# First products of a hybrid encoder layer: low parts on VectorE in order of need, K halves of both units in turn, the queries' low part in both partition halves

## The chip, the cores and the metric

The kernel runs on one core of a Trainium2 chip. The metric is the time of one execution on the device in microseconds; three executions of the kernel before took 883.92, 884.14 and 884.91 us (median 884.14). The core has TensorE (PE, matrix products; its weight loads are a row of their own, PEld), VectorE (DVE), ScalarE (ACT), GpSimd (POOL) and SyncE (SP), which here only issues DMAs. Each engine works through its own instructions in order, and semaphores order them against each other.

## The reference

One encoder layer over 512 positions of width 1024. The normalised input h is multiplied once by a wide matrix `w_in` whose columns feed four token mixers (a short convolution, a stick-breaking attention, an RWKV-7 recurrence, a gMLP gate) and four gates; the sum of the gated mixers goes through `w_o`, and a gated feed-forward part with a short convolution follows. Cut to what matters here:

```python
def stick_breaking_attention(q, k, v):
    ...
        z = jnp.einsum('bhqd,bhkd->bhqk', qi, kh).astype(jnp.float32) * scale
    ...

def hybrid_mixer(h, w_in, ...):
    proj = h @ w_in
    y_a = short_conv_mixer(proj[..., SC_OFF:SB_OFF], sc_conv_w)
    q, k, v = jnp.split(proj[..., SB_OFF:RW_OFF], 3, axis=-1)
    y_b = stick_breaking_attention(q.reshape(hs), k.reshape(hs), v.reshape(hs))
    y_c = rwkv7_mixer(proj[..., RW_OFF:SG_OFF], ...)
    y_d = spatial_gating(proj[..., SG_OFF:GATE_OFF], sg_ln_g, sg_ln_b, sg_w, sg_b)
    ...

def reference(x, mix_norm_g, w_in, ...):
        h = rms_norm(x, mix_norm_g[l])
        x = x + hybrid_mixer(h, w_in[l], ...)
        h = rms_norm(x, ffn_norm_g[l])
        x = x + conv_glu_ffn(h, w_up[l], ffn_conv_w[l], w_down[l])
    return rms_norm(x, final_norm_g)
```

Everything is float32.

## The kernel before

**Products in three parts.** Each operand is split into a high part (`whi`, `hH`: the value cast to a shorter form) and a low part (`wlo`, `hL`: the value less its high part). `mm3` (lines 168 to 172) makes a product of three matmuls: high x high (L169), high x low (L170), low x high (L171), and then calls `tick()`. The cast of `split` (L100) stands on ACT, the difference (L101) on DVE unless another engine is named.

**Weights.** A unit is 256 columns of a weight matrix with all 1024 rows (K). It comes in four pieces of 128 partitions x 512 numbers; piece n holds the rows of K tiles 2n and 2n + 1. SP issues the DMAs in program order (`raw`), ACT and DVE make `whi` and `wlo`.

**First products.** x is 4 tiles of 128 positions (tile 0 to 3). `mix_stats` makes the row sums of squares on ACT in two halves (L181), their sum (L185), root (L187) and inverse (L189). For tiles 0 and 1, PE transposes x against a diagonal of the inverses (L287); `mix_gain` multiplies the result by the norm's weights (`hf`, L238, DVE), and `split` makes hH and hL from it, K half by K half (half 0 is K tiles 0 to 3). For tiles 2 and 3, ACT scales x first (`xn`, L305), and the thread `mix_rest` transposes it later (L314) between the products: `WN` = 19 ticks after the start for tile 2, `WN2` = 5 more for tile 3. `gemm2_halves` multiplies two units, `first` (columns RW0 + 768) and `second` (RW0 + 256 and RW0), first with tiles 0 and 1 (t2_ = 0), then with tiles 2 and 3; in each token half all of the first unit's K comes ahead of the second unit's. The low parts of the first unit's four pieces are made on POOL (`split(*first[0][0], pool)` and so on), all others on DVE.

The order on PE is the program's; in the block around these lines (`manual_schedule` with three engines) so it is on ACT and DVE, except that instructions from outside the block may be put between. Everything else on ACT, DVE and POOL is ordered by the scheduler of the language.

**Queries, keys and scores.** For a pair j of heads, `qS[j]` holds the scaled high part of the queries of head hp in both partition halves, `kS[j]` the high part of the keys in the head's own half and their low part in the other one, so that one matmul of 128 rows gives high x high and low x high (L931). `qL[j]` holds the queries' low part in the own half alone, and a matmul of 64 rows adds high x low (L932); a third one of 128 columns adds the mask (L933). These twelve matmuls of a head, over 512, 384, 256 and 128 columns, are its score block; there are four.

## Time and profile before

| | |
|---|---|
| median of three executions | 884.14 us |
| the profiled execution | 885.09 us |
| its span, first to last instruction | 883.4 us |
| PE busy | 865.9 us (98%) |
| DVE / ACT / POOL busy | 506.0 / 413.2 / 18.9 us |
| mean granted clock of TensorE | 0.992 |

The span is what the trace shows; the execution has 1.7 us around it. Matmuls overlap, so a row's duration is longer than the distance to the next row's start, and distances of starts are what counts on PE. The granted clock is 1.00 at the higher of TensorE's two levels (2.4 GHz) and 0.50 at the lower (1.2 GHz).

### The profile page before, as it was taken

What the parts mean: (1) busy time and instruction counts of PE and PEld (TensorE: products, weight loads), DVE (VectorE), ACT (ScalarE), POOL (GpSimd) and SP (SyncE); (2) the same over time, 40 slices, a digit from 0 to 9 for tenths busy, and PEclk for the clock granted to TensorE, in tenths of its full rate; (3) what the DMA queues carried; (4) which work ended last, traced back from release to release, by engine and by line L of the source; (5) the groups of instructions that cost most, each with busy time, mean ns of one, the idle gap of its engine ahead of it and who ended that gap; (6) DMA issues with size and microseconds to landing.
All of it is one profiled execution on the core that took longest, in us unless ns stands there. A gap on an engine that the chain in (4) does not pass through costs nothing.

```text
span 883.4 us, 12631 instructions
## 1 busy us (share of the span) xinstructions
PE 865.9 (98%) x4767; PEld 709.8 (80%) x4767; DVE 506.0 (57%) x868; ACT 413.2 (47%) x676; POOL 18.9 (2%) x61
## 2 busy tenths in 40 slices
PE   6999999999999999999999999999999999999997
PEld 6978877788778788888888898888888888888876
DVE  5577747875364555544554676634665366634645
ACT  7473345643344587765344554413443144413425
POOL 6000000000000000000000000000000000000000
PEclk9999999999999999999999999999999999999999
DMA  7223331233133322226336252314432063314102
GB/s 242 63 83 99 86 97 49 63 87 97 52 86 93 99 62 65 73 62 200 96 96 182 69 167 96 96 37 117 134 96 84 8 183 107 96 37 131 36 1 95
DMA packets 102773, 82.20 MB, mean 93 GB/s; under 512 B 12716, under 2 KB 92152, under 8 KB 102712
## 3 DMA queue, kind: packets, MB, share of 16 engines
q1 hardware_dynamic: 102040, 79.82, 30.4%
q10 hardware_dynamic: 592, 1.31, 0.5%
q8 instruction: 37, 0.61, 0.3%
q0 software_dynamic: 80, 0.26, 0.1%
q14 instruction: 24, 0.20, 0.1%
HBM read 78.88 MB, written 2.49 MB: 92 GB/s over the span
## 4 chain that ended last, share of the span: by engine, by line
PE 87%; DMA 5%; DVE 4%; ACT 2%; issue 1%; SPq 1%; POOL 0%; ACTq 0%; DVEq 0%
PE mm L169 24%; PE mm L170 24%; PE mm L171 24%; PE wk L169 2%; PE wk L171 2%; PE wk L170 2%; PE wk L552 1%; PE wk L952 1%; DMA raw<-in_w_o_dram 1%; DMA raw<-in_w_in_dram 1%; DMA raw<-in_w_up_dram 1%; DVE wlo L101 1%; DMA x<-in_x_dram 1%; ACT whi L100 1%; PE wk L932 1%
## 5 line engine op out<-in xcount | busy, mean ns | idle before, releaser
L100 ACT CAST whi<-raw 128x512 fp32r<-128x512 f32 x276 | 169.1, 620 | 305.0 <-PE mm L170 148.3
L101 DVE TENSOR_TENSOR wlo<-raw,whi 128x512 fp32r<-128x512 f32 x272 | 185.4, 688 | 172.2 <-ACT whi L100 168.9
L169 PE MATMUL mm<-hH,whi 128*128 128x512 f32 (+1 forms) x448 | 174.3, 389 | 0.9 <-ACT hH L100 0.9
L171 PE MATMUL mm<-hH,wlo 128*128 128x512 f32 (+1 forms) x448 | 169.9, 379 | 3.6 <-POOL wlo L101 3.6
L170 PE MATMUL mm<-hL,whi 128*128 128x512 f32 (+1 forms) x448 | 169.7, 379 | 1.0 <-DVE hL L101 0.9
L170 PE MATMUL mm<-h2L,whi 128*128 128x512 f32 (+1 forms) x368 | 141.0, 383 | 0.5 <-DVE h2L L101 0.5
L169 PE MATMUL mm<-h2H,whi 128*128 128x512 f32 (+1 forms) x368 | 141.2, 384 | 0.1
L171 PE MATMUL mm<-h2H,wlo 128*128 128x512 f32 (+1 forms) x368 | 140.9, 383 | 0.0
L171 PEld LDWEIGHTS mm<-hH,wlo 128*128 128x128 f32 x448 | 85.9, 192 | 19.6 <-POOL wlo L101 3.8
L169 PEld LDWEIGHTS mm<-hH,whi 128*128 128x128 f32 x448 | 85.9, 192 | 18.2 <-issue 1.5
L170 PEld LDWEIGHTS mm<-hL,whi 128*128 128x128 f32 x448 | 85.9, 192 | 15.1 <-DVE hL L101 1.4
L170 PEld LDWEIGHTS mm<-h2L,whi 128*128 128x128 f32 x368 | 69.3, 188 | 14.8 <-DVE h2L L101 0.7
L169 PEld LDWEIGHTS mm<-h2H,whi 128*128 128x128 f32 x368 | 69.3, 188 | 14.5 <-ACT h2H L100 0.3
L171 PEld LDWEIGHTS mm<-h2H,wlo 128*128 128x128 f32 x368 | 69.3, 188 | 14.2
L171 PE MATMUL mm<-whi,aL 128*128 128x512 f32 (+1 forms) x92 | 35.8, 389 | 0.0
L169 PE MATMUL mm<-whi,aH 128*128 128x512 f32 (+1 forms) x92 | 35.7, 388 | 0.0
L170 PE MATMUL mm<-wlo,aH 128*128 128x512 f32 (+1 forms) x92 | 35.7, 388 | 0.0
L169 PE MATMUL wk<-whi,aH 128*128 128x512 f32 (+1 forms) x88 | 34.1, 388 | 0.0
L171 PE MATMUL wk<-whi,aL 128*128 128x512 f32 (+1 forms) x88 | 34.1, 387 | 0.0
L170 PE MATMUL wk<-wlo,aH 128*128 128x512 f32 (+1 forms) x88 | 34.1, 387 | 0.0
L1061 DVE SCALAR_TENSOR_TENSOR ga<-mm,vecs,ga 128x511 f32<-128x511 f32 x22 | 16.5, 749 | 26.4 <-ACT ga L1060 26.4
L1060 ACT ACTIVATE ga<-mm,vecs 128x512 f32<-128x512 f32 x22 | 15.1, 688 | 26.5 <-PE mm L171 26.5
(347 smaller groups left out, 1196.4 us busy)
## 6 DMA issues: line engine op xcount, KB each, us to landing
raw<-in_w_in_dram SPq DMA_DIRECT2D x104, 256.0 KB
raw<-in_w_up_dram SPq DMA_DIRECT2D x176, 128.0 KB
raw<-in_w_down_dram SPq DMA_DIRECT2D x44, 256.0 KB
raw<-in_w_o_dram SPq DMA_DIRECT2D x16, 256.0 KB
x<-in_x_dram SPq DMA_DIRECT2D x4, 512.0 KB
raw<-in_w_in_dram SPq DMA_DIRECT2D x16, 128.0 KB
xt<-in_x_dram SPq DMA_DIRECT2D x4, 512.0 KB
out_dram<-xn SPq DMA_DIRECT2D x4, 320.0 KB
```

Of the source, the lines that this page charges most:

```text
L100: act.copy(hi, src)
L101: eng.tensor_tensor(out=lo, in0=src, in1=hi.bitcast(F32), op=ALU.subtract)
L169: pe.matmul(ps, lhsT=sh, rhs=mh, start=first, stop=False)
L170: pe.matmul(ps, lhsT=sh, rhs=ml, start=False, stop=False)
L171: pe.matmul(ps, lhsT=sl, rhs=mh, start=False, stop=last)
L552: pe.matmul(ps[us, i * 64:i * 64 + 64], lhsT=lt, rhs=rh, start=True, stop=True)
L932: pe.matmul(zreg(si), lhsT=kS[j][own, hp, si * P:(si + 1) * P], rhs=qL[j][own, si * P:T], start=False, stop=False)
L952: pe.matmul(reg, lhsT=lt, rhs=s_[:, OFF[sj]:OFF[sj] + W[sj]], start=False, stop=(sj == 3 and n == 1), skip_group_check=True)
L1060: act.activation(out=t0, in_=ps, func=AF.Copy, scale=ffc(2, i))
L1061: vec.scalar_tensor_tensor(out=t0[:, 1:T], in0=ps[:, 0:T - 1], scalar=ffc(1, i), in1=t0[:, 1:T], op0=ALU.mult, op1=ALU.add)
```

## The change

In the first products the low parts of all weights are made on DVE, in the order in which PE needs them; the row sums of tiles 1 to 3 are one ACT instruction each, and x's tile 0 comes in two DMAs. In each token half PE takes K tiles 0 to 3 of the first unit, then of the second, and then K tiles 4 to 7 of both. `WN` and `WN2` rise, so tile 2's transposes stand after 21 groups of three matmuls (before: 20) and tile 3's after 31 (before: 25), of 32 in the first token half. In the attention `qL` gets the low part in both partition halves, and its matmul takes all 128 rows, which adds low x low to the scores; four DVE instructions of 64 x 512 are added for it. `lo_of` is now one function with its arguments in another order (its other callers are left out here).

```diff
--- before.py
+++ after.py
@@ -33,8 +33,8 @@
 YA, YB, YC, YD, YE, YF, YG, YH = 6, 16, 32, 20, 15, 5, 11, 3
 Y1 = 3
 YS = 2
-WN = 19
-WN2 = 5
+WN = 20
+WN2 = 10
 ND = 3
 FN = 4
 NWARM = 12
@@ -86,7 +89,8 @@
 
     def load_x(tt):
         xx = npool.tile([P, D], F32, tag="x0", name="x0", bufs=4)
-        sp.dma_start(out=xx, in_=x[0, tt * P:(tt + 1) * P, :])
+        for cols in ((half_of(0), half_of(1)) if tt == 0 else (slice(0, D),)):
+            sp.dma_start(out=xx[:, cols], in_=x[0, tt * P:(tt + 1) * P, cols])
         x0.append(xx)
 
     load_x(0)
@@ -96,9 +100,12 @@
     ident = const.tile([P, P], F32, name="ident")
     make_identity(nc, ident)
 
-    def split(src, hi, lo, eng=vec):
+    def lo_of(src, hi, lo):
+        vec.tensor_tensor(out=lo, in0=src, in1=hi.bitcast(F32), op=ALU.subtract)
+
+    def split(src, hi, lo):
         act.copy(hi, src)
-        eng.tensor_tensor(out=lo, in0=src, in1=hi.bitcast(F32), op=ALU.subtract)
+        lo_of(src, hi, lo)
 
 
     wslots = [(wA, NRA, NWA)] * NWA
@@ -174,15 +181,14 @@
     hH = hpool.tile([P, KT, T], F32R, tag="hH", name="hH")
     hL = hpool.tile([P, KT, T], F32R, tag="hL", name="hL")
 
...
     def norm_sums(ss, xs, sq, hf):
         act.activation(out=sq[:, half_of(hf)], in_=xs[:, half_of(hf)], func=AF.Square, accum_out=ss[:, hf:hf + 1])
 
-    def norm_factor(ss):
-        s1 = small.tile([P, 1], F32, tag="s1", name="s1")
-        vec.tensor_tensor(out=s1, in0=ss[:, 0:1], in1=ss[:, 1:2], op=ALU.add)
+    def norm_factor(ss, parts=2):
+        s1 = ss[:, 0:1]
+        if parts == 2:
+            s1 = small.tile([P, 1], F32, tag="s1", name="s1")
+            vec.tensor_tensor(out=s1, in0=ss[:, 0:1], in1=ss[:, 1:2], op=ALU.add)
         rt = small.tile([P, 1], F32, tag="rt", name="rt")
         act.activation(out=rt, in_=s1, func=AF.Sqrt, scale=1.0 / D, bias=eps)
         rs = small.tile([P, 1], F32, tag="rs", name="rs")
@@ -226,11 +232,17 @@
     gT_mix = npool.tile([P, KT, 1], F32, name="gT_mix")
     mix_rs, mix_pt = {}, {}
 
-    def mix_stats(tt):
+    def mix_sums(tt):
         ss, sq, _ = norm_start(npool)
-        for hf in range(2):
-            norm_sums(ss, x0[tt], sq, hf)
-        mix_rs[tt] = norm_factor(ss)
+        if tt == 0:
+            for hf in range(2):
+                norm_sums(ss, x0[tt], sq, hf)
+        else:
+            act.activation(out=sq, in_=x0[tt], func=AF.Square, accum_out=ss[:, 0:1])
+        return ss
+
+    def mix_factor(tt, ss):
+        mix_rs[tt] = norm_factor(ss, 2 if tt == 0 else 1)
 
     def mix_gain(tt, half):
 
@@ -277,7 +289,7 @@
     sp.dma_start(out=stackB, in_=fcw[0:P])
     with tc.manual_schedule(engines={mybir.EngineType.PE, mybir.EngineType.Activation, mybir.EngineType.DVE}):
         for tt in range(2):
-            mix_stats(tt)
+            mix_factor(tt, mix_sums(tt))
             dg = npool.tile([P, P], F32, tag="diag", name="diag", bufs=2)
             vec.tensor_scalar(out=dg, in0=ident, scalar1=mix_rs[tt], scalar2=None, op0=ALU.mult)
             for half in range(2):
@@ -287,22 +299,40 @@
                     pe.matmul(pt[:, k * P:(k + 1) * P], lhsT=x0[tt][:, ks], rhs=dg, start=True, stop=True)
         vec.tensor_copy(gT_mix, warm[:, P:P + KT].rearrange("p (k o) -> p k o", o=1))
         mix_xn = {}
-        s0 = mix_gain(0, 0)
-        split(*first[0][0], pool)
-        split(*first[1][0], pool)
-        act.copy(s0[1], s0[0])
-        s1 = mix_gain(1, 0)
-        split(*first[2][0], pool)
-        split(*first[3][0], pool)
-        vec.tensor_tensor(out=s0[2], in0=s0[0], in1=s0[1].bitcast(F32), op=ALU.subtract)
-        split(*s1)
-        s0, s1 = mix_gain(0, 1), mix_gain(1, 1)
-        split(*s0)
-        split(*s1)
-        for tt in range(2, 4):
-            mix_stats(tt)
+
+
+        def mix_norm(tt, ss):
+            mix_factor(tt, ss)
             mix_xn[tt] = npool.tile([P, D], F32, tag="xn", name="xn", bufs=2)
             act.mul(mix_xn[tt], x0[tt], mix_rs[tt])
+
+        w = [raw_hi_lo for raw_hi_lo, _ in (first[0], first[1], second[0], second[1], first[2], first[3], second[2], second[3])]
+        for n in range(2):
+            act.copy(w[n][1], w[n][0])
+        s0 = mix_gain(0, 0)
+        act.copy(s0[1], s0[0])
+        lo_of(*w[0])
+        s1 = mix_gain(1, 0)
+        act.copy(s1[1], s1[0])
+        lo_of(s0[0], s0[1], s0[2])
+        lo_of(s1[0], s1[1], s1[2])
+        lo_of(*w[1])
+        ss2 = mix_sums(2)
+        split(*w[2])
+        split(*w[3])
+        for n in (4, 5):
+            act.copy(w[n][1], w[n][0])
+        s0, s1 = mix_gain(0, 1), mix_gain(1, 1)
+        act.copy(s0[1], s0[0])
+        act.copy(s1[1], s1[0])
+        lo_of(s0[0], s0[1], s0[2])
+        lo_of(s1[0], s1[1], s1[2])
+        lo_of(*w[4])
+        lo_of(*w[5])
+        mix_norm(2, ss2)
+        split(*w[6])
+        split(*w[7])
+        mix_norm(3, mix_sums(3))
 
     def mix_rest():
         yield WN
@@ -316,8 +346,6 @@
             yield WN2
 
     spawn("norm", mix_rest())
-    for raw_hi_lo, _ in second:
-        split(*raw_hi_lo)
 
     vecs = const.tile([P, 2 * P], F32, name="vecs")
 
@@ -350,11 +378,12 @@
         ps = [[bank(), bank()] for _ in units]
         for t2_ in range(2):
             t_ = slice(256 * t2_, 256 * t2_ + 256)
-            for u, pu in zip(units, ps):
-                for ci, kt in [(ci, kt) for h in range(4) for ci in range(2) for kt in range(2 * h, 2 * h + 2)]:
-                    hi, lo = u[kt // 2]
-                    cs = slice(ci * P, (ci + 1) * P)
-                    mm3(pu[ci][:, t_], hi[:, kt % 2, cs], lo[:, kt % 2, cs], hH[:, kt, t_], hL[:, kt, t_], kt == 0, kt == KT - 1)
+            for hs in ((0, 1), (2, 3)):
+                for u, pu in zip(units, ps):
+                    for ci, kt in [(ci, kt) for h in hs for ci in range(2) for kt in range(2 * h, 2 * h + 2)]:
+                        hi, lo = u[kt // 2]
+                        cs = slice(ci * P, (ci + 1) * P)
+                        mm3(pu[ci][:, t_], hi[:, kt % 2, cs], lo[:, kt % 2, cs], hH[:, kt, t_], hL[:, kt, t_], kt == 0, kt == KT - 1)
             if t2_ == 0:
                 between()
         return ps
@@ -871,22 +900,20 @@
     apool, ast = open_pool("apool", "right")
 
 
+
     HS = [slice(0, 64), slice(64, P)]
     qS, qL, kS, vS = [], [], [], []
-
-    def lo_of(out, src, hi):
-        vec.tensor_tensor(out=out, in0=src, in1=hi.bitcast(F32), op=ALU.subtract)
 
     pss2 = gemm2(col_unit(w_in_v, SB0))
     for j in range(2):
         ps = pss2[j]
         qs = apool.tile([P, 2, T], F32R, tag="qS", name="qS", bufs=2)
-        ql = apool.tile([P, T], F32R, tag="qL", name="qL", bufs=2)
+        ql = apool.tile([P, 2, T], F32R, tag="qL", name="qL", bufs=2)
         for hp in range(2):
             own, oth = HS[hp], HS[1 - hp]
-            act.mul(qs[own, hp, :], ps[own, :], 0.125)
-            act.mul(qs[oth, hp, :], ps[own, :], 0.125)
-            vec.scalar_tensor_tensor(out=ql[own, :], in0=ps[own, :], scalar=0.125, in1=qs[own, hp, :].bitcast(F32), op0=ALU.mult, op1=ALU.subtract)
+            for to in (own, oth):
+                act.mul(qs[to, hp, :], ps[own, :], 0.125)
+                vec.scalar_tensor_tensor(out=ql[to, hp, :], in0=ps[own, :], scalar=0.125, in1=qs[own, hp, :].bitcast(F32), op0=ALU.mult, op1=ALU.subtract)
         qS.append(qs)
         qL.append(ql)
     pss2 = gemm2(col_unit(w_in_v, SB0 + 256))
@@ -929,7 +956,7 @@
 
                 for si in range(4):
                     pe.matmul(zreg(si), lhsT=kS[j][:, hp, si * P:(si + 1) * P], rhs=qS[j][:, hp, si * P:T], start=(si != 3), stop=False)
-                    pe.matmul(zreg(si), lhsT=kS[j][own, hp, si * P:(si + 1) * P], rhs=qL[j][own, si * P:T], start=False, stop=False)
+                    pe.matmul(zreg(si), lhsT=kS[j][:, hp, si * P:(si + 1) * P], rhs=qL[j][:, hp, si * P:T], start=False, stop=False)
                     pe.matmul(zreg(si)[:, 0:P], lhsT=ident_r, rhs=neg_r, start=False, stop=(si != 1))
                 yield Y1
                 az = apool.tile([P, 1280], F32, tag="az", name="az", bufs=2)
```

On DVE, in the first products: `hf_233` and `hf_235` belong to K half 1 of tiles 0 and 1, `wlo_134` to `wlo_149` are the low parts of the second unit's four pieces, `rs_250` is tile 2's factor. Before:

```order
L101 TENSOR_TENSOR hL_94<-hf_224,hH_93 128x4x128
L238 TENSOR_TENSOR hf_233<-mm_188,gT_mix_111 128x512
L238 TENSOR_TENSOR hf_235<-mm_211,gT_mix_111 128x512
L101 TENSOR_TENSOR wlo_134<-raw_132,whi_133 128x512
L101 TENSOR_TENSOR hL_94<-hf_233,hH_93 128x4x128
L101 TENSOR_TENSOR hL_94<-hf_235,hH_93 128x4x128
L101 TENSOR_TENSOR wlo_139<-raw_137,whi_138 128x512
L185 TENSOR_TENSOR s1_246<-ss_241 128x1
L101 TENSOR_TENSOR wlo_144<-raw_142,whi_143 128x512
L189 RECIPROCAL rs_250<-rt_248 128x1
```

In the changed program the same stretch of DVE, where `wlo_119`, `wlo_123` and `wlo_127` are of the first unit (pieces 1 to 3), `wlo_135` to `wlo_150` of the second, `hf_237` and `hf_239` are K half 1 of tiles 0 and 1, and `rs_249` is tile 2's factor:

```order
L104 TENSOR_TENSOR hL_95<-hf_221,hH_94 128x4x128
L104 TENSOR_TENSOR wlo_119<-raw_117,whi_118 128x512
L104 TENSOR_TENSOR wlo_135<-raw_133,whi_134 128x512
L104 TENSOR_TENSOR wlo_140<-raw_138,whi_139 128x512
L250 TENSOR_TENSOR hf_237<-mm_189,gT_mix_112 128x512
L250 TENSOR_TENSOR hf_239<-mm_209,gT_mix_112 128x512
L104 TENSOR_TENSOR hL_95<-hf_237,hH_94 128x4x128
L104 TENSOR_TENSOR hL_95<-hf_239,hH_94 128x4x128
L104 TENSOR_TENSOR wlo_123<-raw_121,whi_122 128x512
L104 TENSOR_TENSOR wlo_127<-raw_125,whi_126 128x512
L195 RECIPROCAL rs_249<-rt_247 128x1
L104 TENSOR_TENSOR wlo_145<-raw_143,whi_144 128x512
```

The two first pieces of the second unit now stand ahead of K half 1 of the tiles, and the low parts of the first unit's upper pieces, which were POOL's, behind it; tile 2's factor follows them.

On ACT, tiles 2 and 3 in the program before (`x0_128` is tile 2, `x0_130` tile 3; `hf_353` is tile 2's K half 0, `whi_614` of the unit after these two):

```order
L187 ACTIVATE rt_248<-s1_246,eps_80 128x1
L100 CAST whi_148<-raw_147 128x512
L305 ACTIVATE xn_252<-x0_128,rs_250 128x1024
L181 ACTIVATE sq_255,ss_254<-x0_130 128x512 x2
L187 ACTIVATE rt_261<-s1_259,eps_80 128x1
L305 ACTIVATE xn_265<-x0_130,rs_263 128x1024
L100 CAST hH_93<-hf_353 128x4x128
L100 CAST hH_93<-hf_362 128x4x128
```

And in the changed one (`x0_129` is tile 2, `x0_131` tile 3; `hf_348` and `hf_357` are tile 2's K halves, `whi_606` is of the unit after):

```order
L193 ACTIVATE rt_247<-ss_227,eps_80 128x1
L307 ACTIVATE xn_251<-x0_129,rs_249 128x1024
L107 CAST whi_144<-raw_143 128x512
L107 CAST whi_149<-raw_148 128x512
L241 ACTIVATE sq_258,ss_257<-x0_131 128x1024
L193 ACTIVATE rt_261<-ss_257,eps_80 128x1
L107 CAST hH_94<-hf_348 128x4x128
L107 CAST whi_606<-raw_605 128x512
L307 ACTIVATE xn_265<-x0_131,rs_263 128x1024
L107 CAST hH_94<-hf_357 128x4x128
```

Tile 3's square sum stood right behind tile 2's `xn`; now two casts of weights stand between them, and two more casts between tile 3's root and its `xn`.

On DVE, tile 3 in the changed program, ahead of the second token half (`hf_396` and `hf_405` are its K halves, `wlo_613` is of the unit after):

```order
L104 TENSOR_TENSOR hL_95<-hf_357,hH_94 128x4x128
L250 TENSOR_TENSOR hf_396<-wk_391,gT_mix_112 128x512
L250 TENSOR_TENSOR hf_405<-wk_400,gT_mix_112 128x512
L104 TENSOR_TENSOR wlo_613<-raw_611,whi_612 128x512
L104 TENSOR_TENSOR hL_95<-hf_396,hH_94 128x4x128
```

Before, the row of these five was the same, with the two `hL` of tile 2 one behind the other ahead of it; what moved is PE's transposes, which tile 3's `hf` wait for.

## Rows read from the trace of the kernel before

**Rows 1.** The page, part 1: busy time, share of the span, instructions.
```profile
PE 865.9 (98%) x4767; PEld 709.8 (80%) x4767; DVE 506.0 (57%) x868; ACT 413.2 (47%) x676; POOL 18.9 (2%) x61
```
**Rows 2.** Waits of PE over the span: us in total, times, longest.
```profile
PE mm L171 <- POOL wlo L101: 3.6, 1, 3.6
PE wk L552 <- DVE Dm L541: 2.2, 1, 2.2
```
**Rows 3.** Timeline, 10 to 21 us: start, duration, instruction [idle before, releaser].
```profile
10.54 1.27 POOL L101 TENSOR_TENSOR wlo<-raw,whi 128x512 fp32r<-128x512 f32 x1
10.59 1.76 DVE L297 TENSOR_TENSOR hL<-hf,hH 128x512 fp32r<-128x512 f32 x1
11.73 0.38 PE L169 MATMUL mm<-hH,whi 128*128 128x256 f32 x1 [0.90 <-ACT hH L100]
12.64 0.62 ACT L100 CAST whi<-raw 128x512 fp32r<-128x512 f32 x1 [0.96 <-DMA raw<-in_w_in_dram]
13.05 0.38 PE L170 MATMUL mm<-hL,whi 128*128 128x256 f32 x1 [0.93 <-DVE hL L101]
14.12 0.68 DVE L101 TENSOR_TENSOR wlo<-raw,whi 128x512 fp32r<-128x512 f32 x1
17.91 1.15 ACT L305 ACTIVATE xn<-x,rs 128x1024 f32<-128x1024 f32 x1 [0.17 <-DVE rs L189]
18.77 2.49 POOL L101 TENSOR_TENSOR wlo<-raw,whi 128x512 fp32r<-128x512 f32 x2
20.09 0.58 PE L171 MATMUL mm<-hH,wlo 128*128 128x256 f32 x1 [3.62 <-POOL wlo L101]
```
**Rows 4.** Stretches: length; busy us of PE, PEld, DVE, ACT, POOL; clock; DMA share, GB/s.
```profile
20.00:25.60 5.60, 5.51 (x26) 5.51 (x27) 1.12 (x2) 1.73 (x4) 1.39 (x5) 0.50 0.33 111
...
311.60:320.00 8.40, 8.40 (x38) 6.95 (x39) 2.60 (x5) 6.93 (x8) 0.00 (x0) 1.00 0.11 33
...
380.60:384.00 3.40, 3.40 (x10) 2.63 (x11) 0.44 (x1) 2.94 (x4) 0.00 (x0) 0.52 0.00 0
```
**Rows 5.** Timeline of PE in the first products.
```profile
21.75 0.41 PE L169 MATMUL mm<-hH,whi 128*128 128x256 f32 x1
21.96 0.41 PE L170 MATMUL mm<-hL,whi 128*128 128x256 f32 x1
...
29.40 1.04 PE L314 MATMUL wk<-ident,xn 128*128 128x128 f32 x8
...
32.91 0.28 PE L170 MATMUL mm<-hL,whi 128*128 128x256 f32 x1
33.02 0.28 PE L171 MATMUL mm<-hH,wlo 128*128 128x256 f32 x1
```
**Rows 6.** Timeline of PE around the fourth score block.
```profile
376.20 0.39 PE L964 MATMUL wk<-aH,vS 128*128 128x512 f32 x1
376.43 0.39 PE L964 MATMUL wk<-aL,vS 128*128 128x512 f32 x1
...
377.42 0.44 PE L931 MATMUL wk<-qS,kS 128*128 128x512 f32 x1
377.79 0.50 PE L932 MATMUL wk<-qL,kS 64*128 64x512 f32 x1
378.22 0.33 PE L933 MATMUL wk<-neg_r,ident_r 128*128 128x128 f32 x1
...
380.59 0.58 PE L169 MATMUL mm<-hH,whi 128*128 128x512 f32 x1
```
**Rows 7.** Timeline of PEld and PE at the first score block.
```profile
308.77 0.18 PEld L932 LDWEIGHTS wk<-qL,kS 64*128 64x128 f32 x1 [0.36 <-issue]
...
311.58 0.45 PE L169 MATMUL mm<-hH,whi 128*128 128x512 f32 x1
311.63 0.19 PEld L170 LDWEIGHTS mm<-hL,whi 128*128 128x128 f32 x1
```
**Rows 8.** The line of the queries' low part: duration min/median/max in ns, starts.
```profile
L889 DVE SCALAR_TENSOR_TENSOR qL<-mm,qS x4: 682/689/696, 284.4 to 289.4; 64x512 fp32r<-64x512 f32 x4
```

More of the change, by code (lines that the diff above doesn't have):

```diff
@@ L73, in bank, with half_of @@
         return psum.tile([P, 512], F32, tag=tag, name=tag, bufs=4)
+    def half_of(hf):
+        return slice(512 * hf, 512 * hf + 512)
     npool, nst = open_pool("npool", "right")
@@ L175, in hybrid_encoder_layer @@
     hL = hpool.tile([P, KT, T], F32R, tag="hL", name="hL")
-    def half_of(hf):
-        return slice(512 * hf, 512 * hf + 512)
     def norm_sums(ss, xs, sq, hf):
         act.activation(out=sq[:, half_of(hf)], in_=xs[:, half_of(hf)], func=AF.Square, accum_out=ss[:, hf:hf + 1])
-    def norm_factor(ss):
-        s1 = small.tile([P, 1], F32, tag="s1", name="s1")
-        vec.tensor_tensor(out=s1, in0=ss[:, 0:1], in1=ss[:, 1:2], op=ALU.add)
+    def norm_factor(ss, parts=2):
[3 more added lines that the diff above has]
+            vec.tensor_tensor(out=s1, in0=ss[:, 0:1], in1=ss[:, 1:2], op=ALU.add)
         rt = small.tile([P, 1], F32, tag="rt", name="rt")
@@ L898, in hybrid_encoder_layer @@
             act.copy(ks[own, hp, :], ps[own, :])
-            lo_of(ks[oth, hp, :], ps[own, :], ks[own, hp, :])
+            lo_of(ps[own, :], ks[own, hp, :], ks[oth, hp, :])
         kS.append(ks)
@@ L913, in hybrid_encoder_layer @@
             act.copy(vs[:, hp, :, own], src)
-            lo_of(vs[:, hp, :, oth], src, vs[:, hp, :, own])
+            lo_of(src, vs[:, hp, :, own], vs[:, hp, :, oth])
         vS.append(vs)
```

## The prediction, made before the changed kernel was run

> **What bounds the kernel now.** I read the page first: TensorE (PE) is busy for 865.9 of 883.4 us [rows 1], so an edit counts by what it takes off PE, or off PE's few waits. The list of PE's waits came next: the longest, 3.6 us, is for a low part of a weight that GpSimd (POOL) makes, and the next is 2.2 us in the RWKV branch [rows 2]. The timeline of the start shows how the first one comes about [rows 3]: the first products begin at 11.73, their second matmul at 13.05 after a wait for hL, and from about 16.4 to 20.09 PE does nothing, because POOL turns to the low parts of the first unit's upper pieces only at 18.77. The table of stretches shows the price behind the wait [rows 4]: from 20 to 25.6 the granted clock is 0.50, the lower of the two levels, and matmuls of 256 columns stand 0.21 us apart (21.75 to 21.96) instead of 0.11 (32.91 to 33.02) [rows 5]. Last I read the attention's score block, since the diff makes its low-part matmul 128 rows high: twelve matmuls take from 377.42 to 380.59, 3.17 us [rows 6], and the weight-load queue shows why [rows 7].
>
> **Part 1, the first products.** The changed program gives PE the first K halves of both units (48 matmuls) before the second halves, puts all low parts on VectorE (DVE) and sends tile 2 and tile 3 through later. I follow the new order with today's durations: 0.68 us for a DVE difference or product of 512 columns, 0.62 for a ScalarE (ACT) cast, 1.15 for xn, 0.115 from one 256-column matmul to the next (half of the 0.23 between the two of 512 columns at 376.20 and 376.43) [rows 3, 6].
>
> (a) Start. Without POOL's difference beside it (10.54), hL costs 0.68 and not 1.76 [rows 3]; with the row sums of x in fewer, earlier steps I put PE's second matmul at 11.5 instead of 13.05. 48 matmuls x 0.115 = 5.5 us bring PE to 17.0. This early start is worth nothing by itself, because the next point doesn't depend on it.
>
> (b) The second unit's first piece lands at 12.64, as it does today (its cast starts then, after 0.96 us of waiting for the DMA) [rows 3]. Its low part starts on DVE at 13.3, and seven more DVE instructions stand in line behind: one low part, two hf, two hL and the two low parts of the first unit's upper half. 13.3 + 7 x 0.68 = 18.1 for the seventh, which PE waits for, 18.8 for the eighth. So PE waits 17.0 to 18.1, in two pieces, instead of until 20.09. What was late on POOL is now late on DVE, by less.
>
> (c) Tile 2. Its factor stands behind the eighth instruction; with xn (1.15) it is ready at 20.1. PE gets to the transposes after 13 more matmuls, 18.1 + 1.5 = 19.6, waits 0.5, spends 0.9 on eight transposes (29.40) [rows 5] and 1.0 on nine matmuls: 22.0.
>
> (d) Tile 3. ACT after 20.1: two casts 1.2, one square sum of 1024 columns about 1.3 (an estimate, twice 0.62, near xn's 1.15), root 0.3, two casts 1.2, xn 1.15: 25.2. PE reaches those transposes after 21 matmuls, 24.5, waits 0.7, and has one group of three matmuls left: 26.4. Then the second token half needs tile 3, and nothing covers it: one cast on ACT to 25.8, and on DVE in line hL, hf, hf, a low part of the next unit, hL: 25.8 + 5 x 0.66 = 29.1. Before, eight groups lay between tile 3's transposes and this point, which hid the same chain.
>
> The third matmul of the second token half, at 33.02 today [rows 5], comes at 29.2: 3.8 us gained. All of the 883 us behind it waits for PE and moves with it. Bounds: no wait after 18.1 would give 3.8 + 0.5 + 0.7 + 2.5 = 7.5; if tile 3 comes 2 us later than worked out, 1.8.
>
> (e) Clock. Half-clock stretches stand behind PE's idle ones: 20 to 25.6 behind the 3.6 us wait, and 380.6 to 384 (0.52) behind a score block [rows 4]. In the new order PE idles 3.2 of the 4.6 us from 24.5 to 29.1, more than in that block, so I charge one such stretch: 3.40 us x (1 - 0.52) = 1.6 us. Bounds: 0, and 2.8 for one as long as today's (5.60 x 0.50). Today's stretch lies ahead of 33.02, so its end is in the 3.8 already. Net of part 1: 2.2.
>
> **Part 2, the score block.** The 64-row matmul becomes a 128-row one with the same columns; nothing else in the block changes. Today the 64-row weight load at 308.77 follows 0.36 us in which its queue issued nothing, whereas a full-height load at 311.63 starts under the matmul of 311.58 [rows 7]. L931 to L932 to L933 takes 0.37 + 0.43 us at 512 columns [rows 6], where two full-height ones would take 0.46. A yardstick with full height alone is the run of eight L964 matmuls just ahead of the block: 512, 512, 384, 384, 256, 256, 128, 128 columns, exactly those of the eight score matmuls, in 377.42 - 376.20 = 1.22 us [rows 6]. Four mask matmuls of 128 columns at 0.11 add 0.44, and I add 0.05 for the last 128-column pair, which alternates with them: 1.71. Saved: 3.17 - 1.71 = 1.46 per block, x 4 = 5.8 us. Bounds: 0 (height doesn't matter) and 4 x (3.17 - 1.38) = 7.2, if only the block's 3072 columns count at 0.23 per 512.
>
> The stretch of half clock behind the fourth block goes with its cause: 1.6 us [rows 4]. The first block has none behind it (311.6 to 320 at 1.00) [rows 4], so other executions may lose none or two; I count one.
>
> The price is four more DVE instructions of 0.69 us [rows 8], 2.8 us in all, in the query unit. They lie beside the key unit's matmuls, and two other banks are free for those; behind them in DVE's line stand weight low parts, of which three or four are ready ahead of PE. DVE is busy 506 of 883 us [rows 1], so I cost them at nothing, and at 2.8 if that cover is gone.
>
> A rule against this part: the Trainium skill, "TensorE: Matmul & The Clock Gate", Part 3 (The mechanism), says that a weight load overlaps running matmuls only where it goes to another row group. By it the full-height load would overlap nothing, and part 2 would bring 0. The trace disagrees: the load at 311.63 runs under the matmul of 311.58 with the same rows.
>
> **Sum**, against the profiled execution (885.09 us; span 883.4 and 1.7 around it): 885.1 - 3.8 + 1.6 - 5.8 - 1.6 = 875.5. That execution is 0.95 above the median of the runs, 884.14; against the median 874.5, which I forecast.
>
> **Rivals.**
> A. No new half-clock stretch: PE's waits around 24.5 to 29.1 fall so that the clock stays. For it: PE also waited 0.9 us twice at 10.6 to 13.05 without a fall. Against it: the new waits are longer. 874.5 - 1.6 = 872.9.
> B. Part 1 is given back at the RWKV wait [rows 2]. For it: PE already waits there, for a DVE chain, and DVE now does four low parts that POOL did. Against: that chain starts from PE's own products. Then the net 2.2 goes, 876.7; with a longer half-clock stretch there too, 878.3.
> C. A full-height second matmul saves nothing, as the rule says: 874.5 + 5.8 + 1.6 = 881.9. The load row speaks against it.
> D. Slower: DVE, now alone on the low parts, becomes the bound between 13.3 and 29.1 us. Some 19 differences and products lie there; at the 1.76 us that hL took at 10.59, they cost 19 x 1.08 = 20 us more, less about 3 us in which DVE waits: 874.5 + 17 = 891.5. It decides from 1.34 us each, (9.6 + 3) / 19 above 0.68. Against it: with POOL's low parts gone, what slowed hL is gone; at 14.12 a difference took 0.68 [rows 3].
>
> **Chances.** Forecast 0.62, A 0.20, B 0.11, C 0.04, D 0.03. The likeliest case alone spans 872 to 877.5; to hold 8 in 10 with A and B and the bounds of tile 3 and of the clock, 870.5 to 879.5. A measurement of this kernel tells 0.2% (1.8 us) from no change; forecast, A and B all lie further below, and C does too: faster 0.95, same 0.02, slower 0.03.
>
> **What would show it.** In the waits of the changed kernel: none for POOL; short ones for DVE low parts near 18, for xn near 20 and 25, and a longer one for tile 3 ahead of the second token half, whose third matmul starts near 29. The timeline of a score block: 1.7 us, with loads under matmuls. The clock: one stretch of 0.5 near 28 to 32, none near 375. I am wrong in part 1 if that third matmul starts after 31 or before 27, and in part 2 if a block takes over 2.2 us.

## The result and the profile after

Four executions of the changed kernel took 872.94 to 873.79 us, median 873.38; the kernel before, on the same chip in the same rounds, 883.92 to 885.52, median 884.52. The ratio is 0.9873, with an interval of 0.9856 to 0.9890: 11 us faster. The forecast was 874.5 us; the time lies between it and rival A (872.9), nearer to A. The profiled execution took 873.0 us (before 885.09).

The page of the changed kernel answers to [rows 1] with its first part; the second line is the granted clock in 40 slices of the span:

```profile
PE 855.2 (98%) x4767; PEld 703.7 (81%) x4767; DVE 508.9 (58%) x873; ACT 412.7 (47%) x670; POOL 11.2 (1%) x57
...
PEclk9999999999999999999999999999999999999999
```

PE lost 10.7 us of busy time with the same 4767 matmuls, so most of the gain is matmuls that take less long, not waits that went. Where it arises is read by setting the same matmul of both timelines side by side (profiled executions, us from the span's start; lines of the changed kernel lie 7 to 30 further down):

| place on PE | before | after | gained up to here |
|---|---|---|---|
| second matmul of the first products | 13.05 | 13.05 | 0.00 |
| third matmul of the second token half | 33.02 | 29.87 | 3.15 |
| RWKV step that waits for Dm (L552, now L581) | 118.09 | 114.84 | 3.25 |
| a matmul 5 us further on | 122.88 | 118.22 | 4.66 |
| first score block | 308.46 | 303.78 | 4.68 |
| second | 331.40 | 325.24 | 6.16 |
| third | 354.39 | 346.81 | 7.58 |
| fourth | 377.42 | 368.38 | 9.04 |
| a matmul some 15 us behind it | 394.60 | 382.92 | 11.68 |
| last matmul | 877.16 | 865.13 | 12.03 |

So: 3.2 us in the first products, 1.4 behind the RWKV wait, 1.5 in each of four score blocks, another 1.2 behind the fourth.

**First products.** Waits of PE in the changed kernel (us in total, times, longest), for [rows 2]:

```profile
PE wk L581 <- DVE Dm L570: 1.8, 1, 1.8
...
PE mm L177 <- DVE hL L104: 1.1, 2, 0.8
PE mm L176 <- DVE hf L250: 1.1, 1, 1.1
PE mm L176 <- ACT hH L107: 1.0, 1, 1.0
```

No wait for POOL is left; in its place stand three of 0.8 to 1.1 us (of the two for hL, the other one, 0.34, is at the start, where before it was 0.93). The timeline of PE shows where (start, duration, instruction, idle before and releaser), for [rows 3, 5]:

```profile
12.32 0.38 PE L176 MATMUL mm<-hH,whi 128*128 128x256 f32 x1 [0.67 <-ACT hH L316]
13.05 0.39 PE L177 MATMUL mm<-hL,whi 128*128 128x256 f32 x1 [0.34 <-DVE hL L104]
...
15.66 0.28 PE L178 MATMUL mm<-hH,wlo 128*128 128x256 f32 x1
17.00 0.35 PE L176 MATMUL mm<-hH,whi 128*128 128x256 f32 x1 [1.06 <-DVE hf L250]
...
21.71 1.04 PE L344 MATMUL wk<-ident,xn 128*128 128x128 f32 x8
...
26.16 1.04 PE L344 MATMUL wk<-ident,xn 128*128 128x128 f32 x8
...
28.50 0.38 PE L176 MATMUL mm<-hH,whi 128*128 128x256 f32 x1 [0.96 <-ACT hH L107]
29.65 0.39 PE L177 MATMUL mm<-hL,whi 128*128 128x256 f32 x1 [0.76 <-DVE hL L104]
29.87 0.28 PE L178 MATMUL mm<-hH,wlo 128*128 128x256 f32 x1
```

Two things to see: behind 24 matmuls PE stops at 15.9 for an `hf`, and tile 3's transposes (26.16) wait for nothing, but what comes after them waits 1.7 us for their result.

**Clock.** The stretches that answer to [rows 4] (length; busy us of PE, PEld, DVE, ACT, POOL; granted clock; DMA): three of after,

```profile
20.00:30.00 10.00, 8.28 (x68) 7.83 (x67) 7.46 (x15) 8.50 (x14) 0.38 (x3) 1.00 0.41 130
30.00:40.00 10.00, 10.00 (x86) 9.95 (x85) 3.80 (x7) 2.42 (x4) 0.00 (x0) 1.00 0.46 129
...
115.00:125.00 10.00, 10.00 (x156) 8.19 (x155) 5.37 (x15) 5.83 (x9) 0.00 (x0) 1.00 0.13 38
```

and one of before that was not shown:

```profile
118.00:121.20 3.20, 3.11 (x35) 2.83 (x36) 1.15 (x2) 1.08 (x2) 0.00 (x0) 0.50 0.27 77
```

Before, the wait for Dm (2.17 us) was followed by half clock from 117.9 to 121.3; after, the wait of 1.77 at the same place, which ends at 114.84, is followed by full clock. That is the 1.4 us of the table.

**Score block.** The fourth one of after, for [rows 6]:

```profile
368.38 0.44 PE L958 MATMUL wk<-qS,kS 128*128 128x512 f32 x1
368.66 0.39 PE L959 MATMUL wk<-qL,kS 128*128 128x512 f32 x1
368.89 0.22 PE L960 MATMUL wk<-neg_r,ident_r 128*128 128x128 f32 x1
368.95 0.40 PE L958 MATMUL wk<-qS,kS 128*128 128x384 f32 x1
...
370.09 0.44 PE L176 MATMUL mm<-hH,whi 128*128 128x512 f32 x1
```

370.09 - 368.38 = 1.71 us, before 3.17; L959 follows L958 after 0.28 instead of 0.37, and L960 follows it after 0.23 instead of 0.43. The weight loads of the first block (PEld), for [rows 7], now each start under the matmul ahead:

```profile
303.78 0.19 PEld L959 LDWEIGHTS wk<-qL,kS 128*128 128x128 f32 x1
304.01 0.19 PEld L960 LDWEIGHTS wk<-neg_r,ident_r 128*128 128x128 f32 x1
```

For [rows 8], six of the eight such instructions on DVE stand in two rows (2.84 us and 1.42; the other two stand by themselves), and PE waits for nothing between 279 and 292:

```profile
281.00 2.84 DVE L916 SCALAR_TENSOR_TENSOR qL<-mm,qS 64x512 fp32r<-64x512 f32 x4
...
284.60 1.42 DVE L916 SCALAR_TENSOR_TENSOR qL<-mm,qS 64x512 fp32r<-64x512 f32 x2
```

### The profile page after: what moved, and what is told of

Same layout as the page of the kernel before. It is cut to its first block, busy times and chain, and to the rows that moved or that the text cites. A ratio compares the mean times of both kernels' runs of the same rounds, so it can differ in the third digit from the quotient of the medians.

```text
span 871.3 us, 12630 instructions
## 1 busy us (share of the span) xinstructions
PE 855.2 (98%) x4767; PEld 703.7 (81%) x4767; DVE 508.9 (58%) x873; ACT 412.7 (47%) x670; POOL 11.2 (1%) x57
## 4 chain that ended last, share of the span: by engine, by line
PE 89%; DVE 4%; DMA 3%; ACT 2%; issue 1%; SPq 0%; ACTq 0%
PE mm L176 25%; PE mm L177 24%; PE mm L178 24%; PE wk L178 3%; PE wk L177 3%; PE wk L176 3%; PE wk L581 1%; PE wk L979 1%; DMA raw<-in_w_in_dram 1%; DVE wlo L104 1%; DMA x<-in_x_dram 1%; PE wk L991 1%; DMA raw<-in_w_up_dram 1%; ACT whi L107 1%; PE wk L525 1%
## 5 line engine op out<-in xcount | busy, mean ns | idle before, releaser
L107 ACT CAST whi<-raw 128x512 fp32r<-128x512 f32 x272 | 166.6, 620 | 305.9 <-PE mm L177 152.7
L104 DVE TENSOR_TENSOR wlo<-raw,whi 128x512 fp32r<-128x512 f32 x276 | 187.9, 689 | 170.8 <-ACT whi L107 170.1
L178 PE MATMUL mm<-hH,wlo 128*128 128x512 f32 (+1 forms) x448 | 168.0, 375 | 0.0
L1087 ACT ACTIVATE ga<-mm,vecs 128x512 f32<-128x512 f32 x22 | 15.1, 687 | 27.1 <-PE mm L178 27.1
```

Of the source, the lines that this page charges most:

```text
L104: vec.tensor_tensor(out=lo, in0=src, in1=hi.bitcast(F32), op=ALU.subtract)
L107: act.copy(hi, src)
L178: pe.matmul(ps, lhsT=sl, rhs=mh, start=False, stop=last)
L1087: act.activation(out=t0, in_=ps, func=AF.Copy, scale=ffc(2, i))
```

## The experiments

Times are medians with the lowest and highest, the ratio that to the kernel before on the same chip (its medians 883.25 to 884.14) with its interval. "Mark" is the start of the third matmul of the second token half (before 33.02, after 29.87), of the profiled execution.

**One part alone.** The changed kernel with the old score block:

```diff
-ql = apool.tile([P, 2, T], F32R, ...)
+ql = apool.tile([P, T], F32R, ...)
...
-    pe.matmul(zreg(si), lhsT=kS[j][:, hp, ...], rhs=qL[j][:, hp, si * P:T], ...)
+    pe.matmul(zreg(si), lhsT=kS[j][own, hp, ...], rhs=qL[j][own, si * P:T], ...)
```

> The changed kernel with the score block as before (64 rows, low part of the queries in one partition half). Theory: the two parts add up. In the two traces the second token half's third matmul comes 3.15 us earlier, the next unit 2.9 us, and the score blocks 1.4 to 1.5 us each shorter; so this kernel should keep some 3 to 3.5 us (881 to 881.5), or up to 5 if it also meets fewer stretches of half clock than before. Score blocks 3.1 to 3.2 us. Rival, the 64-row block isn't the cause and the gain comes from the front alone: 873 to 875.

Measured: 880.66 us (878.10 to 881.89), ratio 0.9969 (0.9954 to 0.9983); mark 29.35, blocks 3.12 and 3.17. The first products alone bring 2.9 us.

The kernel before with the new score block, the same edit the other way:

> The kernel before with the score block of the change alone (the queries' low part in both partition halves, 128 rows). Theory: score blocks of 1.7 us instead of 3.15, four of them, 5.8 us, and 0 to 1.6 us more where a stretch of half clock behind a block goes: 877 to 878.7, wait for POOL's low part still 3.6 us. Rival, a full-height second matmul saves nothing (its weight load overlaps nothing either): 884.5, blocks 3.15 us.

Measured: 874.96 us (874.10 to 879.72), ratio 0.9913 (0.9888 to 0.9937); blocks 1.65 and 1.71. That is 8.6 us below the 883.54 of before, more than the 5.9 that the blocks save; by the interval it may be 5.6 to 9.9. The rest, in the profiled execution, is mostly clock. No half clock stands behind the fourth block or behind the RWKV wait, and in the first products, whose code is that of before, it comes at other times:

```profile
13.40:16.80 3.40, 3.40 (x19) 3.40 (x18) 3.16 (x6) 3.40 (x10) 2.98 (x7) 0.50 0.31 73
20.20:23.70 3.50, 3.50 (x19) 3.50 (x18) 1.07 (x2) 1.44 (x2) 1.00 (x4) 0.51 0.53 170
```

So PE comes to the wait for POOL 1.1 us later than before (17.55 for 16.48) and waits 2.3 us instead of 3.6, while POOL starts on that low part only 0.2 us sooner (18.59 for 18.77). The half clock behind the wait is shorter, and the mark is 31.84. That the edit has a part in this clock is not shown. The two parts, 2.9 and 8.6, add up to 11.5, about the whole change's 11.1.

**Where the first products' start went.** The changed kernel with tile 0 of x in one DMA again; the experiments below that start from it call it the base.

```diff
-for cols in ((half_of(0), half_of(1)) if tt == 0 else (slice(0, D),)):
-    sp.dma_start(out=xx[:, cols], in_=x[0, tt * P:(tt + 1) * P, cols])
+sp.dma_start(out=xx, in_=x[0, tt * P:(tt + 1) * P, :])
```

> The changed kernel with x's tile 0 in one DMA again; its row sums stay in two halves. Theory 1, the split is what delays the loads behind it (tile 1's square sum waits for x until 7.55 instead of finding it there at 6.25, the second unit's first piece is cast at 14.01 instead of 12.64): with one DMA the cast starts near 12.6 again, the first products end 1 to 1.4 us earlier, 872.0 to 872.5. Theory 2, the delay is of that execution and not of the split: cast near 14, time as the changed kernel's, 873.4 within 0.5. Theory 3, the split's earlier first sums are worth something to the end: slower than 873.4 by up to 0.7.

Measured: 873.08 us (871.99 to 873.97), ratio 0.9881 (0.9862 to 0.9900). The timeline of ACT in the changed kernel, with two DMAs,

```profile
3.62 0.63 ACT L185 ACTIVATE sq<-x 128x512 f32<-128x512 f32 x1 [1.32 <-DMA x<-in_x_dram]
...
7.55 1.06 ACT L241 ACTIVATE sq<-x 128x1024 f32<-128x1024 f32 x1 [1.20 <-DMA x<-in_x_dram]
...
14.01 0.62 ACT L107 CAST whi<-raw 128x512 fp32r<-128x512 f32 x1 [0.69 <-DMA raw<-in_w_in_dram]
```

and here, with one:

```profile
4.16 0.63 ACT L184 ACTIVATE sq<-x 128x512 f32<-128x512 f32 x1 [1.85 <-DMA x<-in_x_dram]
...
5.92 1.04 ACT L240 ACTIVATE sq<-x 128x1024 f32<-128x1024 f32 x1
...
12.92 0.62 ACT L106 CAST whi<-raw 128x512 fp32r<-128x512 f32 x1 [0.79 <-DMA raw<-in_w_in_dram]
```

The split brings the first half tile 0.5 us sooner, and tile 1 and the second unit's first piece 1.6 and 1.1 later. It is not of one execution alone: in the kernel with the first products alone, which has the split too, that piece is cast at 13.47, and in the ten profiled executions without the split at 12.64 to 13.17. The second matmul starts at 11.85 (13.05 after), the mark at 28.78. In the time, 0.3 us between the medians is inside the spread of both kernels, and the ratios (0.9881 and 0.9873) lie the other way round; so the gain is shown at the mark alone.

**What the score block's price is.** The kernel before with the block's matmuls in three groups, so that the row height changes twice a block instead of eight times; the 64-row matmuls stay:

```diff
     pe.matmul(zreg(si), lhsT=kS[j][:, hp, ...], rhs=qS[j][:, hp, ...], ...)
+for si in range(4):
     pe.matmul(zreg(si), lhsT=kS[j][own, hp, ...], rhs=qL[j][own, ...], ...)
+for si in range(4):
     pe.matmul(zreg(si)[:, 0:P], lhsT=ident_r, rhs=neg_r, ...)
```

> The kernel before with the twelve matmuls of a score block in another order: the four of 128 rows (high parts), then the four of 64 rows, then the four of the mask; the 64-row matmuls keep their height. Theory 1, the price is in the changes between 64 and 128 rows (eight in a block before, two here): blocks of about 2.0 us, 1.1 less each, 4.5 us in all, 880 (879 to 880.5). Theory 2, each 64-row matmul costs by itself, wherever it stands: blocks of 3.1 us, 884.5.

Measured: 877.76 us (876.84 to 878.36), ratio 0.9933 (0.9916 to 0.9950). The fourth block on PE's timeline:

```profile
371.45 0.80 PE L931 MATMUL wk<-qS,kS 128*128 128x512 f32 x4
372.18 0.84 PE L933 MATMUL wk<-qL,kS 64*128 64x512 f32 x4
372.95 0.66 PE L935 MATMUL wk<-neg_r,ident_r 128*128 128x128 f32 x4
373.45 0.45 PE L169 MATMUL mm<-hH,whi 128*128 128x512 f32 x1
```

2.00 us, against 3.17 with eight changes and 1.71 with none: the price lies in the change of height, not in the half height (0.73 us for the four at 128 rows, 0.77 for the four at 64, with one change of height in each distance). The first block takes 2.43, since its third matmul comes 0.4 us later, behind a wait for DVE (`vS`). The time is below the 879 to 880.5 that were expected: the blocks save 4.2 us, and the median is 5.8 lower. The profiled execution has no half clock behind the RWKV wait or the fourth block either.

**Whether the clock has a part in the front's gain.** The kernel before, with 15 matmuls of ones into a spare bank in PE's wait for POOL (work added, in a bank that nothing reads):

```diff
+for _ in range(fill):
+    pe.matmul(spare[:, 0:P], lhsT=ones_f, rhs=ones_f, start=True, stop=True)
 pe.matmul(pu[ci][:, t_], lhsT=lo[:, 0, cs], rhs=hH[:, kt, t_], ...)
```

> The kernel before with 15 matmuls of ones (128 x 128, about 0.22 us each, 3.3 us in all) into a spare bank put on PE just where it waits for POOL's low part in the first products; the wait itself, 3.6 us until 20.1, stays. Theory, the gain of the front part is almost all clock (the changed front is 3.15 us earlier at the second token half's third matmul in the two traces, and the half-clock stretch behind the wait costs 2.8 us of that): no half clock in the first products, that matmul near 30.3 us where the stretch made it 33.0 (31.7 where it lasted 3.4 us instead of 6.8), time 1.3 to 2.8 us under the kernel before. Rival, the wait is what costs, and the clock is a side effect: as before, within 0.5, or slower by what the 15 matmuls overrun.

Measured: 881.83 us (879.55 to 884.76), ratio 0.9986 (0.9973 to 0.9998). PE's timeline (it has 30 rows for the 15 matmuls) and, apart, the stretches:

```profile
16.15 3.51 PE L362 MATMUL wk<-ones_f 128*128 128x128 f32 x30
19.55 0.39 PE L363 MATMUL mm<-hH,wlo 128*128 128x256 f32 x1
...
30.08 0.28 PE L171 MATMUL mm<-hH,wlo 128*128 128x256 f32 x1
```

```profile
12.00:35.00 23.00, 22.06 (x184) 21.64 (x185) 13.92 (x26) 12.55 (x25) 8.20 (x23) 1.00 0.45 125
117.00:122.00 5.00, 5.00 (x80) 4.16 (x79) 2.65 (x9) 3.25 (x6) 0.00 (x0) 1.00 0.19 56
```

POOL's low part comes nearly as late as before (the matmul that needs it starts at 19.55, before at 20.09), yet the mark comes at 30.08: from there to the mark it takes 10.53 us instead of 12.93. The 2.4 between them is what half clock cost in [rows 4]. So the old order with its clock kept up comes within 0.2 us of the changed kernel's mark (29.87), though 0.5 us of this is POOL's earlier end in that execution: most of what the changed kernel gains at the mark in these executions is clock. In the median the fill brings 1.4 us; its executions lie between 879.55 (the profiled one, mean granted clock 0.999) and 884.76 (0.993).

**What sets the second token half.** On the base, tile 3's transposes 5 ticks earlier:

```diff
-WN2 = 10
+WN2 = 5
```

> The changed kernel with x's tile 0 in one DMA (the base of this and the next two), and WN2 = 5: tile 3's transposes stand after 26 groups of matmuls instead of 31. Theory 1, the start of the second token half is set by the chain on ACT and DVE that makes xn of tile 3, its hf, hH and hL: PE now waits 1.5 us ahead of the transposes and less behind them, third matmul of the second half at the base's 28.8, time within 0.4 of the base (873.1). Theory 2, the distance between transposes and second half sets it: 1.5 to 2 us earlier.

Measured: 873.30 us (871.70 to 874.34), ratio 0.9886 (0.9867 to 0.9906), the base's time. PE's timeline:

```profile
24.70 1.09 PE L343 MATMUL wk<-ident,xn 128*128 128x128 f32 x8 [1.50 <-ACT xn L306]
...
28.33 0.39 PE L176 MATMUL mm<-hL,whi 128*128 128x256 f32 x1 [0.27 <-DVE hL L103]
```

The wait moves from behind the transposes to ahead of them, and the mark from 28.78 to 28.55: the chain of tile 3 on ACT sets it, not PE's order.

On the base, the two `hf` that free PE's banks ahead of the second unit's low parts:

```diff
+s0, s1 = mix_gain(0, 1), mix_gain(1, 1)
 ss2 = mix_sums(2)
...
-s0, s1 = mix_gain(0, 1), mix_gain(1, 1)
 act.copy(s0[1], s0[0])
```

> The base with one edit: the two products hf of tiles 0 and 1, K half 1, stand on DVE ahead of the low parts of the second unit's first two pieces, in the 1.1 us in which DVE waits for those pieces to land, and not behind them. PE's wait of 1.1 us at the second unit's first matmul is put down to such an hf: it holds the bank that this matmul wants. Theory 1, all of DVE's line behind moves up and tile 3's chain with it: that wait gone, third matmul of the second half 1.0 to 1.3 us earlier (27.6), 872. Theory 2, only the wait goes, and PE waits longer later: 873.1 as the base.

Measured: 872.49 us (871.90 to 873.03), ratio 0.9878 (0.9860 to 0.9897). The wait for `hf` (1.06 in the changed kernel) is gone, but the mark, at 28.18, moves by 0.6 only, for the waits for tile 3 stay.

**K halves in turn, or the low parts on DVE?** On the base, PE's old order of K:

```diff
-for hs in ((0, 1), (2, 3)):
+for hs in ((0, 1, 2, 3),):
```

> The changed kernel with x's tile 0 in one DMA (base: third matmul of the second token half at 28.8, 873.1 us) and PE's old order: in a token half all of the first unit's K ahead of the second unit's; DVE's order stays. Theory 1, alternating K halves is what covers DVE's line: PE finishes the first unit's first K half near 14.5 and waits some 3 us, until near 17.6, for the low part of the first unit's third piece, reaches tile 3's transposes near 26.4, and the third matmul of the second half comes at 30.0 to 30.5; with the half-clock stretch that stands behind such a wait 31.5 to 33. Time 1.5 to 4 us over the base. Theory 2, tile 3's chain on ACT and DVE, which doesn't wait for PE until tile 2's transposes, sets the second half in either order: within 0.5 of the base.

Measured: 877.30 us (875.51 to 878.14), ratio 0.9921 (0.9905 to 0.9936), 4.2 above the base (3.6 when each is set against the kernel before of its own rounds). The profiled execution is the slowest of the six. PE's timeline:

```profile
17.05 0.38 PE L175 MATMUL mm<-hH,whi 128*128 128x256 f32 x1 [1.94 <-ACT hH L326]
...
28.86 1.04 PE L343 MATMUL wk<-ident,xn 128*128 128x128 f32 x8
```

PE runs out of ready operands at 15.1, tile 3's transposes come 3.8 us later than in the base (25.07), the mark at 31.84, and half clock is back at 19.1 to 22.5 and 118.1 to 121.5. With all low parts on DVE, the old order keeps most of the old cost: at the mark 3.1 of the 4.2 us between before and the base, half clock included.

On the base, the low parts of the first unit's upper pieces on POOL instead:

```diff
-lo_of(*w[4])
-lo_of(*w[5])
+for n in (4, 5):
+    pool.tensor_tensor(out=w[n][2], in0=w[n][0], in1=w[n][1].bitcast(F32), op=ALU.subtract)
```

> The base with the low parts of the first unit's third and fourth piece on POOL again, where nothing stands ahead of them now; casts and all else as in the base. Theory 1, what was late was POOL's queue order and not its speed, and DVE's line is the longer one now: both low parts ready by 17.6 in either kernel, DVE's line 1.3 us shorter, xn of tile 2 and of tile 3 about 1.2 us earlier, third matmul of the second half near 27.6, 872. Theory 2, POOL's differences slow DVE's (1.76 instead of 0.68 us for the hL beside one in the kernel before), which eats the 1.3: 28.8 and 873, with DVE's differences near 16 us over 1 us each.

Measured: 874.44 us (872.33 to 877.04), ratio 0.9893 (0.9873 to 0.9912). The timeline of POOL and DVE, and the stretch behind the second half's start:

```profile
15.29 2.53 POOL L330 TENSOR_TENSOR wlo<-raw,whi 128x512 fp32r<-128x512 f32 x2 [6.53 <-DMA stackA<-in_rw_r_k_dram]
...
16.70 2.27 DVE L103 TENSOR_TENSOR hL<-hf,hH 128x512 fp32r<-128x512 f32 x2
```

```profile
29.60:33.00 3.40, 3.40 (x18) 3.31 (x17) 0.64 (x2) 0.00 (x0) 0.00 (x0) 0.50 0.28 77
```

Two differences on DVE take 2.27 us beside POOL's two; the pair took 1.29 in the changed kernel. So POOL's help takes away what it gives: the mark is 29.49, and the time, 874.44 against 873.08, is not clear of the spread. And here the half clock behind the second half's waits does occur.

**The version that these point to.** The base with `hf` early, casts and low parts as their pieces land, the factor of each tile made ahead of the casts that it stood behind, and WN2 = 5:

```diff
+s0, s1 = mix_gain(0, 1), mix_gain(1, 1)
+mix_factor(2, mix_sums(2))
...
+split(*w[4])
+split(*w[5])
+mix_scale(2)
+mix_factor(3, mix_sums(3))
 split(*w[6])
 split(*w[7])
-mix_norm(3, mix_sums(3))
+mix_scale(3)
```

> The base with hf as in the run before, casts and low parts of weights and of h alternating as they land, the factors of tiles 2 and 3 made ahead of the weight casts behind them, xn of tile 2 ahead of tile 3's square sum, and WN2 = 5. If the chain of tile 3 on ACT and DVE is what sets the second token half (theory 1), its xn comes some 4 us earlier, near 21, PE runs the first token half with waits under 1 us in all, and the third matmul of the second half comes at 24.5 to 26 instead of 28.8: 869 to 871. If the loads set it, 28 and 872.5.

Measured: **869.13 us** (868.94 to 870.87), ratio 0.9845 (0.9826 to 0.9864), 4.2 us below the changed kernel and 4.0 below the base (3.0 and 3.7 when each is set against the kernel before of its own rounds). PE's timeline:

```profile
21.72 1.04 PE L343 MATMUL wk<-ident,xn 128*128 128x128 f32 x8
...
25.33 0.39 PE L176 MATMUL mm<-hL,whi 128*128 128x256 f32 x1 [0.31 <-DVE hL L103]
```

Tile 3 is 4.4 us earlier than in the changed kernel and 3.4 earlier than in the base, 0.31 of waiting is left ahead of the second half, and the mark is 25.56. The edits were made together; what each of them brings is not shown.

## Why the prediction was right, point by point

**(a) Start.** Wrong in size: 11.5 was forecast, 13.05 came. DVE's hL cost what was worked out (two in 1.46), but the change also splits tile 0's load, and the prediction counted only the row sums of x as fewer, not that the later loads move: one DMA gives 11.85 (the base). Some of the 13.05 is of this execution: the kernel with the first products alone, split too, starts at 12.53. It was called worth nothing by itself, and it was worth little in the time.

**(b) Second unit.** Its first piece was to land at 12.64 as before; its cast starts at 14.01, from the same cause. PE's wait there has another releaser than forecast: the bank of the second unit's first product still holds the transposed x that `hf` reads, so PE stops at 15.9 for 1.06 us. The prediction followed weights and missed a buffer. The forecast end of that wait, 18.1 for a low part, didn't come about: behind `hf`, low parts were there in time.

**(c), (d) Tiles 2 and 3.** Their transposes start at 21.71 and 26.16 without waits (forecast: waits of 0.5 and 0.7), because PE came later; and, as forecast, the second token half then waits for tile 3, 1.72 us in two pieces instead of 2.5. Mark: forecast 29.2, came 29.87, gained 3.15 instead of 3.8, inside the bounds. Part of this closeness is luck, for two misses cancel in part: DVE began on the second unit's low parts 1.4 us late (14.67 for 13.3), but tile 3's xn was ready only 0.8 late (25.96 for 25.2). That tile 3's chain is the last link is shown by the runs with earlier transposes and with the reordered ACT and DVE.

**(e) Clock.** The term that failed. A new half-clock stretch was charged (1.6 us); the profiled execution has none while PE works, as rival A had it, although PE waits 0.96 and 0.76 us there; and the one behind the RWKV wait went too (1.4 us), which the prediction didn't count at all and no edit aimed at. The charge was not baseless: on POOL's variant that stretch is there. Of the 3.15 us of the front, about 2.4 is the old stretch of [rows 4] that went (the fill run); the rest, about 0.75, is earlier work.

**Part 2.** The sum per block, 1.46, came as 1.48, 1.42, 1.46, and the fourth with the half clock behind it as 2.64: 7.0 us where 5.8 + 1.6 = 7.4 was forecast. The yardstick of full-height matmuls gave 1.71 to the hundredth. The rule weighed against it (the Trainium skill, "TensorE: Matmul & The Clock Gate", Part 3, The mechanism) doesn't hold here in the form in which it was weighed: the load at 304.01 starts under the matmul of 304.00, which uses the same rows. The same section also lets a load into the background weight buffer be pulled ahead, which the prediction left out; no run here tells whether that was the case. What does agree is the Trainium skill, "TensorEngine Tiling (Array Packing)", Key Properties: changing the tiling mode drains TensorE. It gives no price; here eight changes cost 3.17 - 1.71 = 1.46 us, about 0.18 each, and two 0.29, about 0.15 each.

**Rivals.** A's condition came true, no new stretch, and the time is nearer to A's. B: the RWKV wait became shorter, 1.8 for 2.2. C falls with blocks of 1.71. D: DVE takes 0.64 to 0.73 per difference in the first products, far below the 1.34 at which it would decide; only beside POOL does it rise, to 1.13.

**The sum.** 885.09 - 3.15 - 1.5 - 7.0 - 0.35 (the rest, spread behind the fourth block) = 873.1. The forecast's sum was 875.5. It charged 1.6 for a stretch that did not come, and left out 1.5 up to the first score block and 0.35 at the end; it promised 0.65 too much in the first products and 0.4 too much in the blocks. So the closeness of 874.5 owes something to errors of both signs. In medians, by the runs with one part alone, part 1 brought 2.9 where its net was 2.2, and part 2 brought 8.6 (5.6 to 9.9) where 7.4 was forecast.

What stays open: why half clock follows the wait for Dm in some profiled executions and not in others; no edit here aimed at that place. The two profiled executions that have it are those with the longest waits there (2.17 and 2.43 us); in the ten without it the wait was 1.62 to 2.14. That the wait is the cause is not shown. Single executions of one kernel differ by the clock too: the kernel with the first products alone took 878.1 us at a mean granted clock of 0.999 and 881.9 at 0.994.

## What to carry to other kernels

Before a matmul of fewer rows is kept among full ones because it "does less", time a run of full-height matmuls with the same columns in the same trace: that yardstick priced a block of this edit to 0.01 us. When operands arrive late, let PE take what is ready of all units first, and follow its banks as well as its operands: the wait moves to the last buffer or tile in line, and the engines that make that one (here ACT's and DVE's order for tile 3) are then worth reordering. Give each half-clock stretch a row of its own in the sum, with both outcomes kept in the range. Before a gain is put down to a wait that went, fill the wait with matmuls that nothing needs: here that showed 2.4 of 3.15 us to be clock.

## What the runs showed of the hardware that was not expected

- Half clock came and went without an edit at its place: behind the RWKV wait it is in the profiled execution of before and of the old K order, and absent in the ten others. In the first products of the kernel with the new score block alone it came at 13.4 to 16.8 us, where the same code in the kernel before had 1.00.
- Matmuls of ones in PE's idle time kept the clock at 1.00 from 12 to 35 us, where it had been 0.50 from 20 to 25.6: 2.4 us less from the end of the wait to the mark, and 1.4 less in the median.
- Splitting one tile's load in two delayed what waits for the next loads: the second unit's first cast starts at 13.47 and 14.01 us in the two profiled executions with the split, at 12.64 to 13.17 in the ten without.
- A half-height matmul is as long as a full one (0.77 us against 0.73 for the four sizes); what costs is the change between heights.
